# A planner's cost table in a two-layer encoder kernel: GpSimd's rotary steps, the date at which a PSUM bank is free, and the rotation's times

## The chip, the core and the metric

The kernel runs on one core of a Trainium2 chip. The metric is device microseconds of one launch. TensorE (PE in the profile) multiplies into PSUM, which has eight banks of 512 float32 per partition here; VectorE (DVE), ScalarE (ACT) and GpSimd (POOL) do the rest, and SyncE (SP) issues most transfers. Each engine works through its own instructions in the order in which they were written.

## The reference

One sequence of 256 tokens with width 1024 goes through two layers. Each layer is: half a SwiGLU step, a mixer, half a SwiGLU step.

```python
x = x + 0.5 * swiglu(rmsnorm(x, ffn1_norm[i]), gate, up, down)       # D_FF = 2816
h = rmsnorm(x, mix_norm[i])
q_s, k_s, v_s, q_m = split(h @ w_in[i])                              # 12 heads of 64, and 4 memory heads
k_m, v_m = split(rmsnorm(mem, mem_norm[i]) @ w_mem_kv[i])
o_m = memory_attention(headnorm(q_m), headnorm(k_m), v_m)            # 256 memory rows
# layer 0: chunked attention with a learned relative bias; layer 1: differential attention
q, k = headnorm(q_s), headnorm(k_s)
if i == 1:
    q, k = apply_rope(q, cos, sin), apply_rope(k, cos, sin)          # cos, sin from int32 positions
    a = softmax(q0 k0) - lam * softmax(q1 k1)
x = x + concat(o_s, o_m) @ w_out[i]
x = x + 0.5 * swiglu(rmsnorm(x, ffn2_norm[i]), gate, up, down)
```

All of it is float32. Sine and cosine of the positions are wanted in layer 1 only.

## The kernel before

**Products.** A float32 product is made of three passes on rounded operands: high by high, high by low, low by high (L596, L599, L602, helper `dense`; the text calls them dense matmuls). Weights come from DRAM in 1 MB pieces into one of three raw buffers (`raw`, L368). ScalarE casts a piece into its high part (`hi`, L417), VectorE subtracts to get the low part (`lo`, L438), 512 columns at a time, into one of four buffers each. A raw buffer is free for the next load only when VectorE has made the last low part of it.

**Stages.** Layer 0: FFN1, then the key and value products of the memory for both layers (`memory_kv`, operands `memh`, `meml`), then mixer 0 (five projections `proj`, attention, output product), FFN2. Layer 1 the same with mixer 1 and no memory products. After FFN1 of layer 0 the new x goes into transposed form by a way through DRAM (`prep_dram`: `xb` on VectorE, transfer `xd<-xb`, transfer `xr<-xd`, both issued from ScalarE's queue); elsewhere TensorE transposes it (L632).

**Norms.** The inverse root of a norm is a power on GpSimd (L639): `xr` for a block of x rows, `hf` for heads (4 or 8 columns), `of` for outputs, `mr` for memory rows. `xrh` is half of `xr`. The head norm (`head_norm`) is a square on ScalarE (`sq`, L1118), a sum and a scaling on VectorE, the power, and one product on VectorE (`qkn` for q and k, `kmn` for memory keys), which TensorE then transposes. The bias tiles of layer 0 get a memset on GpSimd (L1431) once their load is there.

**The rotary table.** `rope_setup` works out cos and sin of position times frequency. The argument is reduced by 92 small GpSimd steps on 128x64 tiles in `ropew` (L1328 to L1336 in a chain, each needing the one before). Two sines on ScalarE follow (L1367, L1368), then sixteen small products on VectorE (L1377, L1379) into `ropeC` and `ropeS`. An Exp of the lambda sums (`le`, L1407) stands behind the sines, and `nlam` on VectorE behind it. In layer 1, `qk_evac` rotates each block: two GpSimd products (L1471), one VectorE product (L1474), one sum (L1478, tile `m`), transposes.

**What sets the order.** The program is written by a planner that runs at build time. `Flow` keeps a clock `now`, which TensorE's instructions advance, and for ScalarE, VectorE and GpSimd (A, V, G) the time at which each will be free. Stages are generators: each writes an instruction, charges its engine with a duration (`flow.act`, `flow.dve`, `flow.pool`), and yields the time at which the result will be there, 0.14 us (`HOP_E`) behind the charge; it is taken up again when the clock has passed that time. So the charges decide where in each engine's order an instruction is written, and nothing else: on the chip, semaphores see to the real dependencies. `Banks` hands out PSUM banks; a stage that wants one waits until one is free. `g2` and `g4` are pools of SBUF tiles that work alike. A function table is loaded on ScalarE (ACT_TABLE_LOAD) where the function in use changes set; `table_hint` (L1111) does this early for Silu and Exp.

Of the kernel before, what the change touches and what calls it, by code (L numbers as in the profile page):

```python
# [12 lines left out]
F32 = mybir.dt.float32  # L13
# [7 lines left out]
P = 128  # L21
# [29 lines left out]
class Flow:  # L51
# [1 line left out]


    def __init__(self):
        self.now = 0.0
        self.free = {"A": 0.0, "V": 0.0, "G": 0.0}
        self.threads = []
        self.idle = []
# [6 lines left out]
        return self.now + HOP  # L66

    def eng(self, e, dur):
        self.free[e] = max(self.free[e], self.now) + dur
        return self.free[e] + HOP_E  # L70

    def act(self, n, extra=0.0):
# [35 lines left out]

    def _advance(self, limit=None):
        c = [th[0] for th in self.threads + self.idle if not callable(th[0])] + list(self.free.values())  # L110
        c = [t for t in c if t > self.now]
        if limit is not None:
            c.append(limit)
        assert c, "no step left to take"
        self.now = min(c)
# [55 lines left out]
class Banks:  # L171

    def __init__(self, tile):
        self.tile, self.free, self.held = tile, list(range(8)), {}

    @property
    def left(self):
        return len(self.free)  # L180

    def has(self, n=1):
        return lambda: len(self.free) >= n

    def has_pair(self):
        return lambda: any(b + 1 in self.free for b in self.free)

    def _hold(self, view, bs):
        for b in bs:
            self.free.remove(b)  # L190
        self.held[id(view)] = (view, bs)
        return view

    def take(self, shape):
        b = self.free[0]
        n = math.prod(shape[1:])
        view = self.tile[:, b, 0:n]
        if len(shape) == 3:
            view = view.rearrange("p (a c) -> p a c", a=shape[1])
        return self._hold(view, (b,))  # L200

    def take_pair(self):
        age = self.free.index
        b = min((b for b in self.free if b + 1 in self.free), key=lambda b: max(age(b), age(b + 1)))
        return self._hold(self.tile[:, b:b + 2, :], (b, b + 1))

    def give(self, view):
        self.free += self.held.pop(id(view))[1]


@with_exitstack
def kernel(
# [13 lines left out]
    flow = Flow()  # L226
# [8 lines left out]
    pp = ctx.enter_context(tc.tile_pool(name="pp", bufs=1, space=PSUM))  # L235

    dram = ctx.enter_context(tc.tile_pool(name="dram", bufs=4, space=bass.MemoryType.DRAM))
    banks = Banks(pp.tile([P, 8, 512], F32, name="banks"))
    g4 = Slots(flow, gp, "g", 12)
    g2 = Slots(flow, t2, "t", NT2)  # L240
    ctx.enter_context(tc.manual_schedule())
# [487 lines left out]
    def prep_rstd(xt, tb):  # L729
        s = small([P, 1], "sst")  # L730
        nc.vector.tensor_add(s, xt.ss[tb][:, 0:1], xt.ss[tb][:, 1:2])
        flow.dve(1, 0.15)
        yield from rsqrt(xt.r[tb], s, 1, 1.0 / D)
        xt.rt[tb] = flow.now
        nc.gpsimd.tensor_scalar(out=xt.rh[tb], in0=xt.r[tb], scalar1=0.5, scalar2=None, op0=ALU.mult)
        flow.pool(0.25)

    final = []

# [565 lines left out]
    def rope_setup():  # L1305
        n = 64
        pi = const.tile([P, 2], I32, name="pos_i")
        later(pi, positions[0].rearrange("(b p) -> p b", p=P))
        invf = const.tile([P, 32], F32, name="invf")
        later(invf, inv_freq.partition_broadcast(P))  # L1310
        gq = const.tile([P, 2, HD], F32, name="gqk")
        later(gq[:, 0], b_q_norm[0].partition_broadcast(P))
        later(gq[:, 1], b_k_norm[0].partition_broadcast(P))
        yield from loaded()
        yield g2.has()
        w = g2.take([P, 8, n], F32, "ropew")
        ang, hi, lo, acc, a, b, fa, cs = (w[:, i, :] for i in range(8))
        pf = const.tile([P, 2], F32, name="pos_f")
        nc.gpsimd.tensor_copy(pf, pi)
        yield flow.pool(0.25)  # L1320
        for tb in range(2):
            nc.gpsimd.tensor_scalar(out=ang[:, tb * 32:(tb + 1) * 32], in0=invf, scalar1=pf[:, tb:tb + 1],
                                    scalar2=None, op0=ALU.mult)
            yield flow.pool(0.25)
        hr = const.tile([P, n], F32R, name="ropehr")
        nc.scalar.copy(out=hr, in_=ang)
        yield flow.act(n)
        nc.gpsimd.tensor_copy(hi, hr.bitcast(F32))  # L1328
        yield flow.pool(0.25)
        nc.gpsimd.tensor_sub(lo, ang, hi)  # L1330
        yield flow.pool(0.25)

        def frac(dst, src):
            nc.gpsimd.tensor_scalar(out=b, in0=src, scalar1=MAGIC, scalar2=MAGIC, op0=ALU.add, op1=ALU.subtract)  # L1334
            yield flow.pool(0.25)
            nc.gpsimd.tensor_sub(dst, src, b)  # L1336
            yield flow.pool(0.25)

        left = Fraction(TWO_PI_INV_NUM, TWO_PI_INV_DEN)
        first = True  # L1340
        for piece in range(5):
            e2 = 14 + 12 * piece
            cval = Fraction(round(left * (1 << e2)), 1 << e2)
            left -= cval
            for part in (hi, lo):
                nc.gpsimd.tensor_scalar(out=a, in0=part, scalar1=float(cval), scalar2=None, op0=ALU.mult)
                yield flow.pool(0.25)
                nc.gpsimd.tensor_scalar(out=fa, in0=a, scalar1=2.0 ** -12, scalar2=MAGIC, op0=ALU.mult, op1=ALU.add)
                yield flow.pool(0.25)
                nc.gpsimd.tensor_scalar(out=fa, in0=fa, scalar1=MAGIC, scalar2=4096.0, op0=ALU.subtract, op1=ALU.mult)  # L1350
                yield flow.pool(0.25)
                nc.gpsimd.tensor_sub(a, a, fa)
                yield flow.pool(0.25)
                if first:
                    yield from frac(acc, a)
                    first = False
                else:
                    yield from frac(fa, a)
                    nc.gpsimd.tensor_add(acc, acc, fa)
                    yield flow.pool(0.25)  # L1360
                    yield from frac(acc, acc)
        S2PI = 6.283185
        nc.gpsimd.tensor_scalar(out=a, in0=acc, scalar1=0.25, scalar2=None, op0=ALU.add)
        yield flow.pool(0.25)
        yield from frac(a, a)
        sn = fa
        nc.scalar.activation(sn, acc, AF.Sin, scale=S2PI)  # L1367
        nc.scalar.activation(cs, a, AF.Sin, scale=S2PI)  # L1368
        sines.append(flow.act(n, 0.3))
        yield sines[0]  # L1370
        for j, sc in ((0, HD ** -0.5), (1, 1.0)):
            for tb in range(2):
                for hf in range(2):
                    own = slice(hf * 32, hf * 32 + 32)
                    oth = slice(32 - hf * 32, 64 - hf * 32)
                    tt = slice(tb * 32, (tb + 1) * 32)
                    nc.vector.scalar_tensor_tensor(out=ropeC[:, tb, j, own], in0=gq[:, j, own], scalar=sc,  # L1377
                                                   in1=cs[:, tt], op0=ALU.mult, op1=ALU.mult)
                    nc.vector.scalar_tensor_tensor(out=ropeS[:, tb, j, own], in0=gq[:, j, oth],  # L1379
                                                   scalar=-sc if hf == 0 else sc,  # L1380
                                                   in1=sn[:, tt], op0=ALU.mult, op1=ALU.mult)
                    flow.dve(n, 0.06)
                    t = flow.dve(n, 0.06) + 0.3
                    yield lambda: flow.now >= t and flow.free["V"] <= flow.now + SLACK
        g2.give()
# [28 lines left out]
    def mixer(l, xt, gc_next):  # L1414
# [34 lines left out]
        class Heads:  # L1449
            def __init__(self):  # L1450
                self.t = [None, None]
                self.k = None

        def qk_evac(c):
            def run(ps, tb, t):
# [5 lines left out]
                if not typ_a:  # L1461
# [6 lines left out]
                    for hf in range(2):  # L1468
# [4 lines left out]
                            in1=ropeS[:, tb, :, own].unsqueeze(2).broadcast_to([P, 2, 4, 32]), op=ALU.mult)  # L1473
                    nc.vector.tensor_tensor(out=m1v, in0=n4,  # L1474
                                            in1=ropeC[:, tb].unsqueeze(2).broadcast_to([P, 2, 4, HD]), op=ALU.mult)
                    flow.dve(512)
                    yield flow.pool(2.1)
                    nc.vector.tensor_add(m1, m1, m2)  # L1478
                    g2.give(2)
                    nat = m1  # L1480
# [5 lines left out]
                else:  # L1486
# [4 lines left out]
                    for j in range(4):  # L1491
                        t = turn(tp[:, j, :], nat[:, j * P:(j + 1) * P])
# [7 lines left out]
                if tb == 0:  # L1500
                    qk.k = g4.take([P, 2, 2, SEQ], F32R, f"k{c}")
                    qk.f = f = g2.take([P, 2, 2, P], F32, f"qk{c}")
                    if typ_a:
# [13 lines left out]
                else:  # L1517
                    qk.q = g2.take([P, 2, 2, P], F32R, f"q{c}")
                    _, t = yield from split_evac(((a4(qk.k[:, 0, :, ts_]), a4(qk.k[:, 1, :, ts_])), tp[:, 2:4], gk),
                                                 ((a4(qk.q[:, 0]), a4(qk.q[:, 1])), tp[:, 0:2], gq))  # L1520
# [110 lines left out]
        def attn_soft(passes, done, vsrc, vready, grp, tb, bias_t, nk):  # L1631
# [5 lines left out]
            for e in range(2):  # L1637
                s, t = ss[e]
# [26 lines left out]
            yield t  # L1665
            rs = small([P, 4], "rs")
            nc.vector.reciprocal(out=rs, in_=sums)
            flow.dve(4)
            pts = [None, None]
            for e in range(2):  # L1670
                pe = pes[e][0]
# [37 lines left out]
        def attn_diff(passes, done, vsrc, vready, grp, tb, nk):  # L1709
# [22 lines left out]
            yield t  # L1732
            rs = small([P, 4], "rs")
            nc.vector.reciprocal(out=rs, in_=sums)
            flow.dve(4, 0.15)
            cf = small([P, 2], "cf")
            nc.vector.scalar_tensor_tensor(out=cf, in0=sums[:, 0:2], scalar=nlam, in1=rs[:, 2:4],
                                           op0=ALU.mult, op1=ALU.mult)
# [288 lines left out]
```

## Time and profile before

| what | value |
|---|---|
| median of 3 runs | 951.9 us (950.87 to 952.27) |
| the profiled execution | 952.73 us |
| its span | 950.8 us |
| busy: TensorE, VectorE, ScalarE, GpSimd | 939.5, 820.6, 582.2, 110.1 us |
| DMA | 209.27 MB, mean 220 GB/s |
| granted TensorE clock, mean | 0.996 |

The span runs from the first to the last instruction; 1.9 us of the execution lie around it. Times in rows of the timeline count from the span's start. A row of the timeline has the start, the length, engine, line, operation and tiles, and in brackets how long the engine was idle before and what ended that. A dense matmul is shown longer (0.39 us) than the distance to the next one, since they overlap, so what matters on TensorE is the distance from start to start.

### The profile page before, as it was taken

What the parts mean: (1) busy time and instruction counts of PE and PEld (TensorE: products, weight loads), DVE (VectorE), ACT (ScalarE), POOL (GpSimd) and SP (SyncE); (2) the same over time, 40 slices, a digit from 0 to 9 for tenths busy, and PEclk for the clock granted to TensorE, in tenths of its full rate; (3) what the DMA queues carried; (4) which work ended last, traced back from release to release, by engine and by line L of the source; (5) the groups of instructions that cost most, each with busy time, mean ns of one, the idle gap of its engine ahead of it and who ended that gap; (6) DMA issues with size and microseconds to landing.
All of it is one profiled execution on the core that took longest, in us unless ns stands there. A gap on an engine that the chain in (4) does not pass through costs nothing.

```text
span 950.8 us, 13163 instructions
## 1 busy us (share of the span) xinstructions
PE 939.5 (99%) x4445; PEld 771.2 (81%) x4445; DVE 820.6 (86%) x1378; ACT 582.2 (61%) x1087; POOL 110.1 (12%) x170
## 2 busy tenths in 40 slices
PE   9999999989999999999999999999999999999998
PEld 7888888767878888888888888888787788888887
DVE  6988969589998889988888999797989888998896
ACT  6655567367777656557645656564677865655661
POOL 1000048522210000000000000000325100000000
PEclk9999999989999999999999999999999999999999
DMA  9877798389746367796747779775632377589651
GB/s 298 271 251 238 233 341 290 122 280 296 242 152 217 124 220 249 238 319 209 229 132 226 235 227 296 242 243 161 218 120 90 102 242 232 184 273 305 219 185 53
DMA packets 176830, 209.27 MB, mean 220 GB/s; under 512 B 12601, under 2 KB 150650, under 8 KB 176762
## 3 DMA queue, kind: packets, MB, share of 16 engines
q1 hardware_dynamic: 168378, 202.92, 65.5%
q10 hardware_dynamic: 8384, 5.51, 1.8%
q8 instruction: 35, 0.57, 0.3%
q14 instruction: 33, 0.27, 0.1%
HBM read 191.62 MB, written 16.78 MB: 219 GB/s over the span
## 4 chain that ended last, share of the span: by engine, by line
PE 76%; DVE 10%; DMA 5%; POOL 5%; issue 2%; ACT 1%; SPq 1%; ACTq 0%; DVEq 0%
PE banks L596 22%; PE banks L602 22%; PE banks L599 22%; DVE lo L438 4%; PE banks L632 2%; PE banks L619 2%; DMA raw<-in_ffn_w_up_dram 2%; POOL ropew L1334 1%; PE banks L1604 1%; PE banks L625 1%; PE banks L1696 1%; POOL ropew L1336 1%; DMA xr<-xd 1%; ACT hi L417 1%; SPq L368 1%
## 5 line engine op out<-in xcount | busy, mean ns | idle before, releaser
L438 DVE TENSOR_TENSOR lo<-raw,hi 128x512 fp32r<-128x512 f32 (+1 forms) x466 | 388.9, 871 | 44.1 <-ACT hi L417 43.8
L417 ACT CAST hi<-raw 128x512 fp32r<-128x512 f32 (+1 forms) x465 | 333.8, 768 | 148.2 <-PE banks L602 68.2
L596 PE MATMUL banks<-hi,xh 128*128 128x512 f32 x736 | 288.8, 392 | 0.0
L599 PE MATMUL banks<-lo,xh 128*128 128x512 f32 x736 | 288.0, 391 | 0.5 <-DVE lo L1921 0.5
L602 PE MATMUL banks<-hi,xl 128*128 128x512 f32 x736 | 287.3, 390 | 0.0
L599 PEld LDWEIGHTS banks<-lo,xh 128*128 128x128 f32 x736 | 138.4, 188 | 29.1 <-DVE lo L1921 1.0
L596 PEld LDWEIGHTS banks<-hi,xh 128*128 128x128 f32 x736 | 138.3, 188 | 28.6
L602 PEld LDWEIGHTS banks<-hi,xl 128*128 128x128 f32 x736 | 138.3, 188 | 28.5
L596 PE MATMUL banks<-hi,ht 128*128 128x512 f32 x270 | 105.4, 390 | 0.0
L599 PE MATMUL banks<-lo,ht 128*128 128x512 f32 x270 | 105.3, 390 | 0.0
L602 PE MATMUL banks<-hi,ht 128*128 128x512 f32 x270 | 105.2, 390 | 0.0
L417 ACT CAST hi<-wsum 128x1024 fp32r<-128x1024 f32 (+1 forms) x51 | 44.6, 890 | 29.6 <-DVE wsum L430 29.4
L639 POOL TENSOR_TENSOR xr<-v,nhalf 128x1 f32<-128x1 f32 x12 | 8.5, 711 | 454.4 <-DVE v L637 454.3
L596 PEld LDWEIGHTS banks<-hi,ht 128*128 128x128 f32 x270 | 50.7, 188 | 10.5
L602 PEld LDWEIGHTS banks<-hi,ht 128*128 128x128 f32 x270 | 50.7, 188 | 10.4
L599 PEld LDWEIGHTS banks<-lo,ht 128*128 128x128 f32 x270 | 50.7, 188 | 10.4
L805 ACT ACTIVATE sil<-banks,xr 128x256 f32<-128x256 f32 x72 | 33.8, 470 | 35.6 <-PE banks L602 33.4
L438 DVE TENSOR_TENSOR lo<-wsum,hi 128x1024 fp32r<-128x1024 f32 (+1 forms) x51 | 50.7, 1021 | 2.9 <-ACT hi L417 2.4
L838 ACT CAST ht<-hr 128x512 fp32r<-128x512 f32 x34 | 21.0, 616 | 34.0 <-DMA hr<-hd 34.0
L639 POOL TENSOR_TENSOR hf<-v,nhalf 128x8 f32<-128x8 f32 (+1 forms) x20 | 32.0, 1598 | 72.6 <-DVE v L637 72.6
L840 DVE TENSOR_TENSOR ht<-hr,ht 128x512 fp32r<-128x512 f32 x34 | 23.4, 688 | 15.9 <-ACT ht L838 15.9
L430 DVE TENSOR_TENSOR wsum<-raw,wsum 128x512 f32<-128x512 f32 (+1 forms) x36 | 32.4, 919 | 0.3
(223 smaller groups left out, 1263.7 us busy)
## 6 DMA issues: line engine op xcount, KB each, us to landing
raw<-in_ffn_w_down_dram SPq DMA_DIRECT2D x176, 256.0 KB, 4.1
raw<-in_ffn_w_gate_dram SPq DMA_DIRECT2D x81, 512.0 KB, 4.3
raw<-in_ffn_w_up_dram SPq DMA_DIRECT2D x81, 512.0 KB, 5.0
raw<-in_w_in_dram SPq DMA_DIRECT2D x32, 512.0 KB, 4.9
hd<-hb SPq DMA_DIRECT2D x44, 256.0 KB, 5.0
hr<-hd SPq DMA_DIRECT2D x44, 256.0 KB, 4.8
raw<-in_w_out_dram SPq DMA_DIRECT2D x8, 1024.0 KB, 4.8
raw<-in_w_mem_kv_dram SPq DMA_DIRECT2D x4, 1024.0 KB, 5.9
```

Source lines behind the costliest of these rows:

```text
L417: nc.scalar.copy(out=it.part(0, q, w), in_=src())
L430: nc.vector.tensor_sub(it.t[j], x(), y())
L438: nc.vector.tensor_sub(it.part(1, q, w), src(), it.part(0, q, w).bitcast(F32))
L596: nc.tensor.matmul(out=ps, lhsT=xh, rhs=wh, start=start, stop=False)
L599: nc.tensor.matmul(out=ps, lhsT=xh, rhs=wl, start=False, stop=False)
L602: nc.tensor.matmul(out=ps, lhsT=xl, rhs=wh, start=False, stop=stop)
L619: nc.tensor.matmul(out=ps, lhsT=xt.h[tb][:, kk, :], rhs=w, start=start and k == i == 0, stop=False)
L632: nc.tensor.transpose(out=dst, in_=src, identity=ident)
L639: nc.gpsimd.tensor_tensor(out=dst, in0=v[:, :n], in1=nhalf[:, :n], op=ALU.pow)
L805: nc.scalar.activation(sil[:, tb], ps[:, tb, 0:256], AF.Silu, scale=xt.r[tb])
L838: nc.scalar.copy(out=hi, in_=src)
L840: nc.vector.tensor_sub(lo, src, hi.bitcast(F32))
```

## The change

Three groups of edits, all in the planner; every engine gets the same arithmetic as before.

1. In `rope_setup`, and for `xrh`, each small GpSimd step is charged 0.56 us instead of 0.25.
2. `Flow` notes the end of the last charge made (`done`). A bank that is given back is free from that date on, not at once, and `free` lists only banks whose date has passed.
3. The rotation in layer 1 is charged 0.35 us more on VectorE and 2.4 instead of 2.1 on GpSimd; two reciprocals 0.1 and 0.3 more.

```diff
     def eng(self, e, dur):
-        self.free[e] = max(self.free[e], self.now) + dur
+        self.done = self.free[e] = max(self.free[e], self.now) + dur
         return self.free[e] + HOP_E
...
-    def __init__(self, tile):
-        self.tile, self.free, self.held = tile, list(range(8)), {}
+    def __init__(self, flow, tile):
+        self.flow, self.tile, self.held = flow, tile, {}
+        self.given = [(b, 0.0) for b in range(8)]
+
+    @property
+    def free(self):
+        return [b for b, t in self.given if t <= self.flow.now]
...
     def give(self, view):
-        self.free += self.held.pop(id(view))[1]
+        self.given += [(b, self.flow.done) for b in self.held.pop(id(view))[1]]
...
         nc.gpsimd.tensor_copy(pf, pi)
-        yield flow.pool(0.25)
+        yield flow.pool(0.56)
...
-                    flow.dve(512)
-                    yield flow.pool(2.1)
+                    flow.dve(512, 0.35)
+                    yield flow.pool(2.4)
...
-            flow.dve(4)
+            flow.dve(4, 0.1)
...
-            flow.dve(4, 0.15)
+            flow.dve(4, 0.45)
```

The first order changes behind the down products of layer 0's FFN1. Line numbers from the banks on are 4 higher after the change (L1367 is L1371, L417 is L421, L632 is L636). Outside the two mixers and the stretch ahead of mixer 0 the rows are the same.

On ScalarE the two sines stood between memory splits (`memh`) and the switch to Exp, ahead of the first split of the memory weights (`raw_1647`):

```order
L417 CAST hi_0_1719<-raw_1565 128x512 x2
L1212 ACTIVATE memh_1713<-mr,gcol 128x256
L1212 ACTIVATE memh_1714<-mr,gcol 128x256 x2
L1367 ACTIVATE ropew<-ropew 128x64
L1368 ACTIVATE ropew<-ropew 128x64
L1111 ACT_TABLE_LOAD
L1111 ACTIVATE dummy<-dummy 128x1
L1212 ACTIVATE memh_1714<-mr,gcol 128x256
L417 CAST hi_0_1793<-raw_1647 128x512
```

Now they stand in mixer 0, between the squares of the first q and k block's two row halves (`sq`), with a table load ahead of them and another ahead of `le`:

```order
L1122 ACTIVATE sq<-banks,xr 128x512
L421 CAST hi_0_2240<-raw_2131 128x512
L1282 ACTIVATE km_1896<-kr,gcol 128x256
L421 CAST hi_0_2240<-raw_2131 128x512
L1282 ACTIVATE km_1896<-kr,gcol 128x256
L421 CAST hi_0_2240<-raw_2131 128x512 x2
L1371 ACT_TABLE_LOAD
L1371 ACTIVATE ropew<-ropew 128x64
L1372 ACTIVATE ropew<-ropew 128x64
L1122 ACTIVATE sq<-banks,xr 128x512
L1411 ACT_TABLE_LOAD
L1411 ACTIVATE le<-le 128x2
```

So the sines and `le` moved past the memory splits, the transfers of the DRAM way and the casts of nine weight pieces.

On GpSimd all rotary steps stood ahead of the first `xr` of mixer 0, and the head norms of the memory and of q and k behind them without a step between:

```order
L1363 TENSOR_SCALAR ropew<-ropew 128x64
L1334 TENSOR_SCALAR ropew<-ropew 128x64
L1336 TENSOR_TENSOR ropew<-ropew 128x64
L639 TENSOR_TENSOR xr<-v,nhalf 128x1
L735 TENSOR_SCALAR xrh<-xr 128x1
L639 TENSOR_TENSOR xr<-v,nhalf 128x1
L735 TENSOR_SCALAR xrh<-xr 128x1
L1431 MEMSET bias_1939 64x4x64
L639 TENSOR_TENSOR hf<-v,nhalf 128x4
L1431 MEMSET bias_2012 64x4x64
```

Now 34 of the steps stand between them; the last rows of the chain are these:

```order
L643 TENSOR_TENSOR hf<-v,nhalf 128x4
L1340 TENSOR_TENSOR ropew<-ropew 128x64
L1363 TENSOR_TENSOR ropew<-ropew 128x64
L1338 TENSOR_SCALAR ropew<-ropew 128x64
L1340 TENSOR_TENSOR ropew<-ropew 128x64
L1367 TENSOR_SCALAR ropew<-ropew 128x64
L1338 TENSOR_SCALAR ropew<-ropew 128x64
L643 TENSOR_TENSOR hf<-v,nhalf 128x8
L1340 TENSOR_TENSOR ropew<-ropew 128x64
L643 TENSOR_TENSOR hf<-v,nhalf 128x8 x5
```

The sines' argument is complete one step behind the first `hf` of 128x8.

On TensorE, late in mixer 0, the transposes of the softmax (`pe`), three groups of attention products (L1696, with `tr` or `PT`) and the memory scores (L1604) stood in one piece inside the output product:

```order
L632 MATMUL banks<-ident,pe 128x128 x16
L1696 MATMUL banks<-tr,V_2292 64x128 x2
L1696 MATMUL banks<-tr,V_2293 64x128 x2
L1696 MATMUL banks<-tr,V_2292 64x128 x2
L1696 MATMUL banks<-tr,V_2293 64x128 x2
L1696 MATMUL banks<-PT,vm_1943 64x128 x8
L1696 MATMUL banks<-PT,V_2292 64x128 x2
L1696 MATMUL banks<-PT,V_2293 64x128 x2
L1696 MATMUL banks<-PT,V_2292 64x128 x2
L1696 MATMUL banks<-PT,V_2293 64x128 x2
L1604 MATMUL banks<-km_1942,qmT 128x256 x12
L596 MATMUL banks<-hi_0_2708,oT_2923 128x512
```

Now the groups stand apart, with dense matmuls between; two of them:

```order
L636 MATMUL banks<-ident,pe 128x128 x4
L1700 MATMUL banks<-PT,vm_1897 64x128 x8
L600 MATMUL banks<-hi_0_2852,oT_2947 128x512
L603 MATMUL banks<-lo_0_2853,oT_2947 128x512
L606 MATMUL banks<-hi_0_2852,oT_2947 128x512
L600 MATMUL banks<-hi_0_2852,oT_2947 128x512
L603 MATMUL banks<-lo_0_2853,oT_2947 128x512
L606 MATMUL banks<-hi_0_2852,oT_2947 128x512
L636 MATMUL banks<-ident,pe 128x128 x4
L1700 MATMUL banks<-PT,V_2275 64x128 x2
L1700 MATMUL banks<-PT,V_2276 64x128 x2
```

The dense matmuls keep their own order; the groups between them moved by a few dense matmuls.

More of the change, by code (lines that the diff above doesn't have):

```diff
@@ L55, in __init__ @@
     def __init__(self):
-        self.now = 0.0
+        self.now = self.done = 0.0
         self.free = {"A": 0.0, "V": 0.0, "G": 0.0}
@@ L110, in _advance @@
         c = [th[0] for th in self.threads + self.idle if not callable(th[0])] + list(self.free.values())
-        c = [t for t in c if t > self.now]
+        c = [t for t in c + [self.done] if t > self.now]
         if limit is not None:
@@ L182, in has @@
     def has(self, n=1):
-        return lambda: len(self.free) >= n
+        return lambda: self.left >= n
     def has_pair(self):
@@ L188, in _hold @@
     def _hold(self, view, bs):
-        for b in bs:
-            self.free.remove(b)
+        self.given = [g for g in self.given if g[0] not in bs]
         self.held[id(view)] = (view, bs)
@@ L194, in take @@
     def take(self, shape):
-        b = self.free[0]
+        b = (self.free or [g[0] for g in self.given])[0]
         n = math.prod(shape[1:])
@@ L202, in take_pair @@
     def take_pair(self):
-        age = self.free.index
-        b = min((b for b in self.free if b + 1 in self.free), key=lambda b: max(age(b), age(b + 1)))
+        free = self.free if self.has_pair()() else [g[0] for g in self.given]
+        b = min((b for b in free if b + 1 in free), key=lambda b: max(free.index(b), free.index(b + 1)))
         return self._hold(self.tile[:, b:b + 2, :], (b, b + 1))
     def give(self, view):
-        self.free += self.held.pop(id(view))[1]
+        self.given += [(b, self.flow.done) for b in self.held.pop(id(view))[1]]
 @with_exitstack
@@ L237 @@
     dram = ctx.enter_context(tc.tile_pool(name="dram", bufs=4, space=bass.MemoryType.DRAM))
-    banks = Banks(pp.tile([P, 8, 512], F32, name="banks"))
+    banks = Banks(flow, pp.tile([P, 8, 512], F32, name="banks"))
     g4 = Slots(flow, gp, "g", 12)
@@ L735, in prep_rstd @@
         nc.gpsimd.tensor_scalar(out=xt.rh[tb], in0=xt.r[tb], scalar1=0.5, scalar2=None, op0=ALU.mult)
-        flow.pool(0.25)
+        flow.pool(0.56)
     final = []
@@ L1323, in rope_setup @@
                                     scalar2=None, op0=ALU.mult)
-            yield flow.pool(0.25)
+            yield flow.pool(0.56)
         hr = const.tile([P, n], F32R, name="ropehr")
@@ L1328, in rope_setup @@
         nc.gpsimd.tensor_copy(hi, hr.bitcast(F32))
-        yield flow.pool(0.25)
+        yield flow.pool(0.56)
         nc.gpsimd.tensor_sub(lo, ang, hi)
-        yield flow.pool(0.25)
+        yield flow.pool(0.56)
         def frac(dst, src):
             nc.gpsimd.tensor_scalar(out=b, in0=src, scalar1=MAGIC, scalar2=MAGIC, op0=ALU.add, op1=ALU.subtract)
-            yield flow.pool(0.25)
+            yield flow.pool(0.56)
             nc.gpsimd.tensor_sub(dst, src, b)
-            yield flow.pool(0.25)
+            yield flow.pool(0.56)
         left = Fraction(TWO_PI_INV_NUM, TWO_PI_INV_DEN)
@@ L1346, in rope_setup @@
                 nc.gpsimd.tensor_scalar(out=a, in0=part, scalar1=float(cval), scalar2=None, op0=ALU.mult)
-                yield flow.pool(0.25)
+                yield flow.pool(0.56)
                 nc.gpsimd.tensor_scalar(out=fa, in0=a, scalar1=2.0 ** -12, scalar2=MAGIC, op0=ALU.mult, op1=ALU.add)
-                yield flow.pool(0.25)
+                yield flow.pool(0.56)
                 nc.gpsimd.tensor_scalar(out=fa, in0=fa, scalar1=MAGIC, scalar2=4096.0, op0=ALU.subtract, op1=ALU.mult)
-                yield flow.pool(0.25)
+                yield flow.pool(0.56)
                 nc.gpsimd.tensor_sub(a, a, fa)
-                yield flow.pool(0.25)
+                yield flow.pool(0.56)
                 if first:
@@ L1359, in rope_setup @@
                     nc.gpsimd.tensor_add(acc, acc, fa)
-                    yield flow.pool(0.25)
+                    yield flow.pool(0.56)
                     yield from frac(acc, acc)
@@ L1363, in rope_setup @@
         nc.gpsimd.tensor_scalar(out=a, in0=acc, scalar1=0.25, scalar2=None, op0=ALU.add)
-        yield flow.pool(0.25)
+        yield flow.pool(0.56)
         yield from frac(a, a)
```

## The prediction

> **What bounds the kernel now.** The page first: how busy each engine is, and in which slices TensorE is not.
>
> ```profile
> span 950.8 us, 13163 instructions
> PE 939.5 (99%) x4445; PEld 771.2 (81%) x4445; DVE 820.6 (86%) x1378; ACT 582.2 (61%) x1087; POOL 110.1 (12%) x170
> PE   9999999989999999999999999999999999999998
> ```
>
> TensorE works nearly all the time, so the change can only win where TensorE stands still or runs slowly; the one low slice inside the span is around 190 us. The table by stretches opens that place (columns: length, then busy us and instruction count of PE, PEld, DVE, ACT, POOL, then granted clock, DMA share, GB/s).
>
> ```profile
> 160.00:170.00 10.00, 10.00 (x45) 8.26 (x44) 10.00 (x24) 8.16 (x18) 8.68 (x17) 1.00 0.76 268
> 170.00:181.00 11.00, 11.00 (x50) 9.12 (x49) 2.87 (x8) 0.52 (x3) 8.88 (x23) 1.00 0.35 131
> 181.00:188.00 7.00, 6.64 (x30) 5.20 (x29) 5.57 (x16) 5.08 (x10) 0.00 (x0) 1.00 0.00 1
> 188.00:200.00 12.00, 8.42 (x25) 6.03 (x25) 11.06 (x28) 6.59 (x16) 0.83 (x2) 0.72 0.88 292
> 200.00:212.00 12.00, 11.08 (x46) 8.22 (x46) 9.37 (x21) 6.96 (x15) 3.60 (x6) 1.00 0.79 242
> 212.00:240.00 28.00, 27.37 (x125) 22.24 (x124) 26.33 (x56) 20.81 (x42) 7.82 (x6) 1.00 0.93 301
> ```
>
> Read down the columns. From 170 to 181 VectorE and ScalarE almost stop while GpSimd alone works; from 181 to 188 the DMA engines carry nothing; from 188 to 200 TensorE loses matmuls and its granted clock falls to 0.72. The waits of ScalarE and VectorE between 160 and 200 say what the first stop was.
>
> ```profile
> ACT ropew L1367 <- POOL ropew L1336: 10.1, 1, 10.1
> DVE ropeC L1377 <- ACT ropew L1368: 8.1, 1, 8.1
> ```
>
> ScalarE reached the sine of the rotary table (L1367) 10.1 us before GpSimd had finished its argument, and everything behind it in ScalarE's order waited: the casts L417 that split the next weights. VectorE sat behind the sines at L1377. Raw buffers came free late, so no load was issued, and TensorE paid last:
>
> ```profile
> 188.79 0.40 PE L602 MATMUL banks<-hi,meml 128*128 128x512 f32 x1
> 191.99 0.79 PE L596 MATMUL banks<-hi,memh 128*128 128x512 f32 x1 [2.81 <-ACT hi L417]
> 193.56 0.79 PE L599 MATMUL banks<-lo,memh 128*128 128x512 f32 x1 [0.77 <-DVE lo L438]
> 194.15 0.63 PE L602 MATMUL banks<-hi,meml 128*128 128x512 f32 x1
> 194.57 0.63 PE L596 MATMUL banks<-hi,memh 128*128 128x512 f32 x1
> ```
>
> After 2.81 us without work the matmuls start 0.42 us apart (194.15 to 194.57), where 45 in 10 us (row 160:170) means 0.22.
>
> **The change, part by part.**
>
> *Rotary steps at 0.56 us instead of 0.25.* The pace GpSimd really had, first and last step before the sines:
>
> ```profile
> 128.91 0.52 POOL L1328 COPY ropew<-ropehr 128x64 f32<-128x64 f32 x1 [14.24 <-ACT ropehr L1326]
> 180.36 0.32 POOL L1336 TENSOR_TENSOR ropew<-ropew 128x64 f32<-128x64 f32 x1
> ```
>
> From the first's start to the last's end are 92 steps (and two short powers for the memory rows) in 51.8 us, 0.56 each. The planner took 0.25 plus its hop of 0.14 per step and so put the sines too early. With 0.56 plus the hop it puts them far later: in the new order they stand behind the first 128x8 `hf` of the first q/k block, in mixer 0, and not before its memory products. No arithmetic is added or removed on GpSimd.
>
> What the stall costs: at the rate of 160 to 181 ((45 + 50) / 21 = 4.52 matmuls a us) the 31 us from 181 to 212 would hold 140; they held 30 + 25 + 46 = 101. 39 missing matmuls are 8.7 us, half-clock time included. I take all of it: **-8.7**. The lower bound is the part before 200 alone: 19 us would hold 86, they held 55, 6.8 us.
>
> Where do the sines block now? In the new order GpSimd has 34 rotary steps left from the mixer's first `xr`, spread between two `xr`, three bias memsets and five `hf` (four of 128x4).
>
> ```profile
> 191.09 0.57 POOL L639 TENSOR_TENSOR xr<-v,nhalf 128x1 f32<-128x1 f32 x1 [10.40 <-DVE v L637]
> 226.97 2.05 POOL L639 TENSOR_TENSOR hf<-v,nhalf 128x8 f32<-128x8 f32 x1 [3.94 <-DVE v L637]
> L639 POOL TENSOR_TENSOR hf<-v,nhalf 128x4 f32<-128x4 f32 x8 | 9.5, 1186 | 28.5 <-DVE v L637 28.5
> 216.56 0.31 POOL L1431 MEMSET bias<- 64x256 f32 x1 [3.63 <-PE banks L602]
> ```
>
> From the start of that `xr` to the end of that `hf` there are 37.9 us. The steps beside a busy VectorE (row 160:170: 17 in 10 us) take 0.59 each, so 34 are 20 us; two `xr` some 1.2, four `hf` 4.8, the long one 2.1, memsets 0.9: 29 us of 37.9. The tightest part is the last: the third memset at 216.56 waits for TensorE, and from there to 226.97, 10.4 us, stand 11 steps (6.5) and two short `hf` (2.4). So the argument is ready about when `hf` is, plus one last step, and ScalarE reaches the sines after four casts and two `km` activations. ScalarE's wait there: 0 to 0.5 us.
>
> New work on ScalarE: in the old order the sines stood before the switch to Exp, now they stand after it, and the new order has two table loads more (before the sine, before `le`).
>
> ```profile
> 181.00 1.28 ACT L1111 ACT_TABLE_LOAD   x1
> 182.29 0.20 ACT L1111 ACTIVATE dummy<-dummy 128x1 f32<-128x1 f32 x1
> 211.90 0.62 ACT L417 CAST hi<-raw 128x512 fp32r<-128x512 f32 x1 [2.34 <-DMA raw<-in_w_in_dram]
> 229.85 0.66 PE L632 MATMUL banks<-ident,qkn 128*128 128x128 f32 x4 [0.63 <-DVE qkn L1127]
> ```
>
> Two loads are 2.6 us, which the planner does not reckon. Their cover is the lead of the splits: at 211.90 a cast came 2.34 us late in this mixer, and TensorE's only wait from 212 to 240 is the 0.63 before L632, which is no wait for a split. If that cover is gone, they cost up to 2.6. `le` now also holds `nlam` on VectorE, with five splits and the second `qkn` queued behind it; that block's transposes keep their place among the dense matmuls. I put **+0.8** for ScalarE's and VectorE's new lateness, between 0 and 2.6, nearer to 0 because the late cast cost nothing. The Trainium skill, "ScalarE: Activation LUTs", section "What ACT_TABLE_LOAD costs", adds about 1.38 us of drain to each load; here the next instruction starts 1.29 after the load's start, so the row decides. By that page the two loads would be about 5.3 us (an estimate), and the sum up to 2.7 us worse.
>
> The 0.63 itself should go: the first `qkn` transposes now stand seven dense matmuls (1.5 us) later. **-0.6**, at worst 0.
>
> *Rotation in layer 1 (512 with 0.35 more on VectorE, 2.4 for the GpSimd pair), reciprocals (+0.1, +0.3).*
>
> ```profile
> PE banks L632 <- DVE m L1478: 0.7, 2, 0.4
> PE banks L632 <- DVE oT L1569: 0.2, 1, 0.2
> L1474 DVE TENSOR_TENSOR m<-qkn,ropeC x6: 685/774/1232, 682.0 to 728.7; 128x512 f32<-128x512 f32 x6
> L1471 POOL TENSOR_TENSOR m<-qkn,ropeS x12: 738/1059/1454, 681.7 to 729.2; 128x256 f32<-128x256 f32 x12
> ```
>
> All waits of TensorE between 660 and 800 are 0.9 us. Two `ropeS` products at 1.06 are 2.1 us and can reach 2.4; the first two rotation transposes move two and one dense matmuls back. That covers the 0.4 and part of the rest: **-0.5**, from 0 to -0.9.
>
> *A bank free when its reader is done.* The only bank wait that could be meant is the 0.2 at L1569. In `finish` and `prep_half` the bank is given back before the reader is charged, so there the date noted is an older instruction's; it does nothing there. What the new dates do is move small groups of products: with fewer banks at once, groups that ran in one piece are run apart. In the new order the dense stream is broken by scores or AV products 12 times instead of 9 in mixer 0, and 15 instead of 12 in mixer 1. One break's price, an AV group (16 by the profile's count) alone and the same inside a run:
>
> ```profile
> 294.53 1.04 PE L1696 MATMUL banks<-PT,vm 128*64 128x128 f32 x16
> 295.41 1.04 PE L1696 MATMUL banks<-PT,V 128*64 128x128 f32 x16
> ...
> 304.96 0.40 PE L602 MATMUL banks<-hi,oT 128*128 128x512 f32 x1
> 305.28 1.09 PE L1696 MATMUL banks<-PT,vm 128*64 128x128 f32 x16
> 306.31 0.50 PE L596 MATMUL banks<-hi,oT 128*128 128x512 f32 x1
> ```
>
> Alone it takes 1.35 from the last dense start to the next, less one dense pitch of 0.22: 1.13, and the dense matmul behind it is 0.1 longer; in the run 0.88. So about 0.3 a break, six of them **+1.8** (0 if the groups' inner waits are the same, 2.1 at 0.35 each).
>
> Sum: -8.7 - 0.6 - 0.5 + 0.8 + 1.8 = **-7.2**. The profiled execution took 952.7 (span 950.8 and 1.9 around it); that gives 945.5. It lies 0.8 above the median of the runs shown, 951.9, so I forecast **944.7** for the median.
>
> **The rivals.**
>
> *The wait only moves.* ScalarE waits for GpSimd again, now in mixer 0. From the sums above it begins where 11 steps fill 10.4 - 2.4 = 8 us, 0.73 a step, and over the whole way at 28.9 / 34 = 0.85, against 0.59 measured beside the busiest VectorE. At 1.0 a step the sines are 5 us late; taking off the 2.3 us of lead seen, TensorE idles about 2.8, the gap after which the clock fell above, and loses another 2 or more there: 4 to 5 us back, **949**.
>
> *The round trip through DRAM is the real limit.* ScalarE's order also holds the issue of `xr<-xd`, which waits until `xd<-xb` has landed.
>
> ```profile
> 190.40 6.12 DMA xd<-xb
> 196.54 7.37 DMA xr<-xd
> ACT hi L417 <- DMA xd<-xb: 2.8, 1, 2.8
> ```
>
> From the chain: 6.1 out and 7.4 back, under the rush of loads after 188. If the four trips hold ScalarE 2.8 each in 176 to 196, some 3 us of the 8.7 stay: **947.7**. Against it: without the stop, the trips start about 10 us earlier and the loads come spread out.
>
> *Slower.* GpSimd's steps delay the `hf` queued behind them. In-order as it is, each `hf` of the memory keys and of q/k stands behind two to six rotary steps. To eat 7.2 us, they would have to run some 7 + 2.3 us late: 38 us for 34 steps, 1.1 us each. The Trainium skill, "GPSIMD Engine Reference", section "Key points", has GpSimd share its SBUF interfaces with VectorE and names VectorE instructions with two SBUF inputs, which the splits L438 are. The trace agrees in kind: 23 operations in 8.88 us busy beside an idle VectorE (row 170:181), 17 in 8.68 beside a full one, 0.39 against 0.51 each; 1.1 lies far above both. Time: **954**.
>
> *It changes nothing.* The planner moves the sines but something else late at 188 holds TensorE, as above: 951.5.
>
> **How the numbers follow.** The forecast has 0.70 (own range 942 to 947.3), the wait that moves 0.09, the round trip 0.11, no change 0.05, slower 0.05. The range holds the forecast, the round trip and most of the moved wait: 941.7 to 949. About 0.2% (1.9 us) is what a measurement here can tell from no change; 0.90 of the cases lie below that, 0.05 within, 0.05 above.
>
> **What would show it.** In the new profile ScalarE's wait at the sine (L1371 there) is under 1 us, DMA has no empty stretch between 170 and 190, and the memory products run from 186 to 208 at 4.5 a us with the clock at 1.00: that is the -8.7. Two more ACT_TABLE_LOAD, 7 in all. More than 1 us of TensorE waits on `qkn`, L421 or L442 between 200 and 235 would spoil the +0.8; as many matmuls a us as before in the rest of both mixers would say that the breaks cost nothing. A wait of ScalarE on GpSimd or on `xd` above 3 us, or a clock below 1.00 after 200, would make the forecast wrong.

## The result, and the profile after

The changed kernel takes 944.43 us (median of 6 runs, 942.75 to 945.40); the kernel before, on the same chip, 952.19 (6 runs, 950.87 to 954.47). The ratio is 0.9912, 95% interval 0.9897 to 0.9927. A second comparison, beside three experiments below, gave 943.11 and 0.9898 (0.9885 to 0.9912). The profiled execution took 944.51 us.

The page first, with the same lines as before:

```profile
span 942.6 us, 13176 instructions
PE 936.2 (99%) x4445; PEld 768.8 (82%) x4445; DVE 821.4 (87%) x1378; ACT 583.5 (62%) x1089; POOL 112.9 (12%) x170
PE   9999999999999999999999999999999999999998
```

The low slice around 190 is gone. The same stretches as in the prediction (length, busy us and count of PE, PEld, DVE, ACT, POOL, granted clock, DMA share, GB/s):

```profile
170.00:181.00 11.00, 11.00 (x50) 9.13 (x49) 9.66 (x21) 4.45 (x11) 5.50 (x14) 1.00 0.59 187
181.00:188.00 7.00, 7.00 (x32) 5.79 (x32) 3.42 (x5) 2.22 (x6) 3.08 (x9) 1.00 0.70 246
188.00:200.00 12.00, 12.00 (x54) 9.94 (x54) 10.10 (x19) 9.15 (x19) 5.93 (x12) 1.00 0.88 284
200.00:212.00 12.00, 11.50 (x50) 8.89 (x49) 11.93 (x25) 7.72 (x16) 7.31 (x12) 1.00 0.77 258
212.00:240.00 28.00, 27.91 (x140) 22.50 (x139) 27.17 (x81) 24.67 (x57) 9.08 (x12) 1.00 0.79 255
```

VectorE works on from 170 to 181, the DMA engines carry 246 GB/s from 181 to 188 where they carried 1, and the clock from 188 to 200 is 1.00 where it was 0.72. Of the waits that the prediction asked about, these are left (total, times, longest):

```profile
ACT ropew L1372 <- POOL ropew L1340: 0.9, 1, 0.9
PE banks L603 <- DVE lo L442: 0.5, 2, 0.3
PE banks L636 <- DVE m L1482: 0.2, 1, 0.2
```

ScalarE waits 0.9 us between the two sines instead of 10.1 ahead of them; TensorE waits on no `qkn`, and 0.2 us on the rotation where its waits between 660 and 800 were 0.9 in all. The profile has seven table loads, as the prediction said.

**Where the time went.** The dense matmuls stand in the same order in all fourteen profiles of this study (thirteen kernels, the changed one twice), so each stage can be timed from the start of its first dense matmul to the start of the next stage's first. The memory products are dense matmuls 780 to 875 (counted from 0), mixer 0 is 876 to 1211, mixer 1 is 2658 to 2993. Every stage outside these took the same in every kernel: 179.4 to 180.2 us ahead (from the first dense matmul), 342.0 between the mixers, 161.6 behind (to the start of the last dense matmul). So the whole study is in this table (us, one profiled execution each).

| kernel | pace | banks | rotation | memory products | mixer 0 | mixer 1 | span |
|---|---|---|---|---|---|---|---|
| before | | | | 30.7 | 111.0 | 114.5 | 950.8 |
| after; again | x | x | x | 22.8; 21.8 | 111.5; 111.2 | 113.7; 113.7 | 942.6; 941.2 |
| p1_pace | x | | | 21.8 | 112.7 | 114.6 | 943.4 |
| p2_banks | | x | | 31.6 | 112.3 | 116.2 | 954.7 |
| p3_rotation | | | x | 27.5 | 111.7 | 116.5 | 950.1 |
| p13_pace_rotation | x | | x | 22.0 | 112.5 | 116.5 | 945.5 |
| late_sines | | | | 22.9 | 110.6 | 114.6 | 942.4 |
| pace40 | 0.40 | x | x | 24.3 | 110.8 | 113.8 | 944.6 |
| four_loads | x | x | x | 25.1 | 116.0 | 113.7 | 949.1 |
| slow_steps | x | x | x | 23.3 | 117.0 | 113.8 | 948.6 |
| sines_ffn2 | x | x | x | 21.8 | 112.2 | 113.8 | 942.1 |
| sines_ffn2_quarter | 0.25 | x | x | 23.6 | 112.0 | 113.8 | 944.1 |
| sines_ffn2_nobanks | x | | x | 23.6 | 112.1 | 116.5 | 946.7 |

The change is -7.9 in the memory products, +0.5 in mixer 0, -0.8 in mixer 1: -8.2 of span (in its second profile -8.9, +0.2 and -0.8). The eleven profiles without the stall spread from 21.8 to 25.1 in the memory products, and the two of one kernel lie 1.0 apart, so a difference of that size in this column says nothing.

### The profile page after: what moved, and what is told of

It is laid out like the page before. It is cut to its first block, busy times and chain, and to the rows that moved or that the text cites. A ratio compares the mean times of both kernels' runs of the same rounds, so it can differ in the third digit from the quotient of the medians.

```text
span 942.6 us, 13176 instructions
## 1 busy us (share of the span) xinstructions
PE 936.2 (99%) x4445; PEld 768.8 (82%) x4445; DVE 821.4 (87%) x1378; ACT 583.5 (62%) x1089; POOL 112.9 (12%) x170
## 4 chain that ended last, share of the span: by engine, by line
PE 92%; DVE 5%; DMA 1%; ACT 1%; issue 1%; POOL 0%; ACTq 0%
PE banks L606 28%; PE banks L600 28%; PE banks L603 28%; PE banks L636 2%; PE banks L623 2%; DVE lo L442 2%; PE banks L1608 1%; PE banks L629 1%; PE banks L1700 1%; DMA xr<-xd 1%; ACT hi L421 0%; POOL hf L643 0%; PE banks L1757 0%; DVE m L1478 0%; DVE hss L1125 0%
## 5 line engine op out<-in xcount | busy, mean ns | idle before, releaser
L442 DVE TENSOR_TENSOR lo<-raw,hi 128x512 fp32r<-128x512 f32 (+1 forms) x466 | 390.6, 873 | 48.9 <-ACT hi L421 48.5
L421 ACT CAST hi<-raw 128x512 fp32r<-128x512 f32 (+1 forms) x465 | 333.8, 768 | 145.5 <-PE banks L606 74.7
L421 ACT CAST hi<-wsum 128x1024 fp32r<-128x1024 f32 (+1 forms) x51 | 44.6, 890 | 28.7 <-DVE wsum L434 28.5
L442 DVE TENSOR_TENSOR lo<-wsum,hi 128x1024 fp32r<-128x1024 f32 (+1 forms) x51 | 50.4, 1020 | 3.1 <-ACT hi L421 2.8
```

The source lines that it names most:

```text
L421: nc.scalar.copy(out=it.part(0, q, w), in_=src())
L442: nc.vector.tensor_sub(it.part(1, q, w), src(), it.part(0, q, w).bitcast(F32))
```

## The experiments

**The parts of the change, one at a time.** Each kernel is the one before with some of the three groups of edits, as in the diff above: the pace alone, the bank dates alone, the rotation and reciprocals alone, and pace with rotation.

> Of the change only the rotary steps at 0.56 us; banks and rotation times as before. Theory (the sines no longer stop ScalarE, and that is the whole gain): 8 us below the kernel before, 944 to 945, sines' wait on ScalarE under 1.5 us, no DMA gap at 181. Rival (the dates of the banks or the rotation's times carry a part): only 5 to 6 us below, 946 to 947. In its order mixer 0 has 12 breaks of the dense stream like the changed kernel, mixer 1 has 12 like the kernel before: if a break costs 0.3 us, this one gains up to 0.9 on the changed kernel in mixer 1.

> Of the change only the dates of the banks; rotary steps at 0.25 and rotation as before. The order has as many breaks as before (9 and 12), so the breaks do not come from the banks, against what the prediction said. Theory: within 1 us of the kernel before, 951 to 953, with the 10 us wait at the sines still there. Rival (bank dates spare TensorE waits of their own): 1 to 2 us faster.

> Of the change only the rotation and reciprocal times. Theory: the waits at the rotation's transposes shrink by 0.5 us, 3 more breaks in mixer 1 and 2 in mixer 0 cost up to 1.5: 951.5 to 953.5. Rival (the breaks cost nothing, the waits go): 0.5 to 1 us faster, 951 to 951.5.

> The change without the dates of the banks. Theory: like the changed kernel within 0.5 us, 944 to 945. Rival (bank dates matter beside the other two): 946 or more.

Measured against the kernel before on the same chip (median 951.79):

| kernel | median | ratio (95%) |
|---|---|---|
| p1_pace | 945.34 | 0.9938 (0.9924 to 0.9952) |
| p2_banks | 955.66 | 1.0045 (1.0028 to 1.0062) |
| p3_rotation | 954.51 | 1.0032 (1.0021 to 1.0043) |
| p13_pace_rotation | 947.66 | 0.9964 (0.9952 to 0.9975) |

The profiled execution of p3_rotation, 951.85 us, is the fastest of its ten, so its row in the table shows its good end. The pace alone is most of the gain; its time lies between what its theory and its rival had. The other two parts, each alone, make the kernel slower, by more than theory or rival had for either. Without the dates the rival came true: they matter beside the other two. The profiles of the pace alone, the banks alone and the rotation alone, in this order, say first that only the pace takes the stall away (where ScalarE still waits 8.3 to 11.2 us at the sine, the memory products take 27.5 to 31.6 us):

```profile
ACT ropew L1368 <- POOL ropew L1336: 0.3, 1, 0.3
```

```profile
ACT ropew L1371 <- POOL ropew L1340: 11.2, 1, 11.2
188.00:200.00 12.00, 7.94 (x24) 5.72 (x25) 11.65 (x28) 5.87 (x14) 0.83 (x2) 0.72 0.82 267
746.65 0.41 PE L636 MATMUL banks<-ident,o 128*128 128x128 f32 x2 [1.59 <-ACT pe L1663]
```

```profile
ACT ropew L1367 <- POOL ropew L1336: 8.3, 1, 8.3
PE banks L632 <- ACT pe L1659: 1.5, 1, 1.5
PE banks L632 <- ACT PT L1618: 0.5, 1, 0.5
```

Their last lines are the second finding. Mixer 1 takes 114.5 or 114.6 in all kernels with neither banks nor rotation, 116.5 in all with the rotation and no dates, 116.2 with the banks alone, and 113.7 or 113.8 in all seven profiles with both: +2.0, +1.7, and together -0.8. The timeline of pace with rotation shows what the rotation brings. First TensorE, then ScalarE:

```profile
733.85 0.40 PE L602 MATMUL banks<-hi,oT 128*128 128x512 f32 x1
735.78 0.44 PE L632 MATMUL banks<-ident,o 128*128 128x128 f32 x2 [1.53 <-ACT pe L1659]
735.97 0.48 PE L596 MATMUL banks<-hi,oT 128*128 128x512 f32 x1
736.28 0.40 PE L599 MATMUL banks<-lo,oT 128*128 128x512 f32 x1
736.52 0.39 PE L602 MATMUL banks<-hi,oT 128*128 128x512 f32 x1
...
741.71 0.66 PE L632 MATMUL banks<-ident,pe 128*128 128x128 f32 x4 [0.50 <-ACT PT L1618]
```

```profile
734.71 0.47 ACT L1659 ACTIVATE pe<-banks,nm 128x256 f32<-128x256 f32 x1
...
735.16 0.47 ACT L1659 ACTIVATE pe<-banks,nm 128x256 f32<-128x256 f32 x1
```

The transposes of `o` do not read `pe`. They write into a bank that the code gives back as soon as the Exp (L1659) is written down (`banks.give(src)` right behind it), and on the chip the Exp runs until 735.6. With the dates on top, the two waits are gone: between 660 and 800 only the 0.2 us of the row above is left. That the dates hand another bank to these transposes is inferred from that. The banks alone still have a wait of 1.59 of the same kind; that a date is only as good as the planned end of the reader would explain it, but no run tests that. In mixer 0, too, the pace alone has a wait of TensorE on an Exp, here at the scores (0.5 with the rotation added); neither profile of the changed kernel has any wait of TensorE there:

```profile
PE banks L1604 <- ACT pe L1659: 0.7, 1, 0.7
```

**The sines late, and nothing else.** The kernel before with one line in `rope_setup`, ahead of the sines; all rotary steps keep 0.25 and their order. The planner writes some later instructions of the other engines in another order too.

```diff
+        yield flow.now + 13.0
         nc.scalar.activation(sn, acc, AF.Sin, scale=S2PI)
```

> The kernel before, with all charges as before, but rope_setup lets 13 us of the planner's clock go by before it writes the two sines, so they stand behind the place where ScalarE waited 10.1 us. Two more table loads, like the changed kernel. Theory (only the sines' place matters, not the pace of the steps or the order of GpSimd): ScalarE's wait at the sine under 2 us, memory products from 185 to about 208, 944 to 946.5. Rival (the stall hangs on GpSimd's steps standing in one block, or on the table load and the way through DRAM): 948 or more.

Measured: 944.73 us, ratio 0.9934 (0.9911 to 0.9958), beside a kernel before of 951.67. The sine in its timeline:

```profile
L1368 ACT ACTIVATE ropew<-ropew x1: 257/257/257, 181.1 to 181.1; 128x64 f32<-128x64 f32 x1
188.00:200.00 12.00, 12.00 (x55) 9.93 (x54) 11.04 (x23) 10.63 (x22) 3.14 (x5) 1.00 0.84 266
```

The first sine starts at 181.1, no earlier than before (179.3, as soon as its argument was there); only, the work that had waited behind it now stands ahead of it, and ScalarE does not wait for GpSimd there. The memory products take 22.9. So the cause of the stall is shown: the sines' place in ScalarE's order, and not the pace as such.

**A smaller pace.** The changed kernel with 0.40 for 0.56 at every step:

```diff
-        yield flow.pool(0.56)
+        yield flow.pool(0.40)
```

> The changed kernel with rotary steps charged 0.40 instead of 0.56. The sines then stand some 20 rows of ScalarE earlier, still behind the memory weights' first casts. Theory (any place later than the argument's real end will do): wait at the sine under 2 us, 944 to 946. Rival (0.56 is needed, the chain is still late): ScalarE waits 3 us or more, 948 or more.

Measured: 943.77 us, ratio 0.9928 (0.9908 to 0.9948). The sines stand at 199.7, without a wait. So 0.56 is not needed: 0.40, too, puts the sines behind their argument.

**Two more table loads.** The changed kernel with two dummy activations behind `le`, which the planner does not reckon:

```diff
         nc.scalar.activation(e, e, AF.Exp)
+        nc.scalar.activation(dummy, dummy, AF.Silu)
+        nc.scalar.activation(dummy, dummy, AF.Exp)
```

> The changed kernel with two more table loads behind le (a Silu and an Exp of one element, not charged to the planner, so that the order of everything else stays). Theory (the splits' lead covers 2.6 us of ScalarE in mixer 0): within 0.7 us of the changed kernel, 944 to 945.2. Rival (no cover left): 2.6 us or more on top, 947 and above, with TensorE waits for L421 or L442 between 215 and 235.

Measured: 947.42 us (10 runs, 945.70 to 951.23), ratio 0.9963 (0.9945 to 0.998). Its profiled execution is the slowest of the ten; 2.1 of its loss lie between 187.9 and 192.7, ahead of the edit, in waits for splits of the memory weights. The other 4.5 us, in mixer 0, are these (ScalarE, VectorE, TensorE):

```profile
226.58 1.28 ACT L1412 ACT_TABLE_LOAD   x1
...
228.10 1.28 ACT L1413 ACT_TABLE_LOAD   x1
...
229.50 2.16 ACT L421 CAST hi<-raw 128x512 fp32r<-128x512 f32 x4
...
230.14 2.50 DVE L442 TENSOR_TENSOR lo<-raw,hi 128x512 fp32r<-128x512 f32 x4 [2.78 <-ACT hi L421]
232.55 0.74 DVE L1131 SCALAR_TENSOR_TENSOR qkn<-banks,xr,hf 128x512 f32<-128x512 f32 x1
...
230.01 0.39 PE L600 MATMUL banks<-hi,xh 128*128 128x512 f32 x1
233.35 1.11 PE L636 MATMUL banks<-ident,qkn 128*128 128x128 f32 x4 [2.96 <-DVE qkn L1131]
...
235.12 0.63 PE L600 MATMUL banks<-hi,xh 128*128 128x512 f32 x1
235.54 0.63 PE L603 MATMUL banks<-lo,xh 128*128 128x512 f32 x1
```

The loads hold four casts, the casts hold four of the five low parts that stand ahead of the second `qkn` on VectorE, and `qkn` holds TensorE for 2.96 us; then the matmuls come 0.42 us apart instead of 0.23. In the changed kernel the same transposes have just no wait:

```profile
227.73 0.74 DVE L1131 SCALAR_TENSOR_TENSOR qkn<-banks,xr,hf 128x512 f32<-128x512 f32 x1
...
228.04 0.39 PE L600 MATMUL banks<-hi,xh 128*128 128x512 f32 x1
228.52 0.66 PE L636 MATMUL banks<-ident,qkn 128*128 128x128 f32 x4
```

`qkn` ends at 228.47 and the transposes start at 228.52, 0.05 later; in four_loads they start 0.06 after the end of theirs (233.29). So nothing was left of the cover here: the two loads of the change fit, and in this execution the next two cost their full length and the clock on top. The rival's time came true, but not its wait: it looked for one of TensorE on a split (L421 or L442), and TensorE waited for `qkn`. Between the medians the price is 3.0 us (947.42 against 944.43), and the fastest of the ten runs is only 1.3 above the changed kernel's median, so 4.5 is not paid every time.

**Every GpSimd step twice.** The changed kernel with a second small step behind nearly every rotary step, without a charge:

```diff
+        nc.gpsimd.tensor_scalar(out=spare, in0=invf, scalar1=0.5, scalar2=None, op0=ALU.mult)
         yield flow.pool(0.56)
```

> The changed kernel with a second small GpSimd product (128x32, into a spare tile, not charged) ahead of each step of the rotary chain's main part, which makes a step 0.95 to 1.1 us instead of 0.56; the order of everything else stays. By the prediction's reckoning the sines are then 5 to 8 us late in mixer 0: ScalarE waits 4 to 8 us there, and the time goes to 948 to 953. Rival (hf and the sines have more room than reckoned): under 946.5.

Measured: 951.44 us, ratio 1.0005 (0.9993 to 1.0017). Its waits from 200 to 240, and TensorE's timeline:

```profile
ACT vm L1258 <- DVE kmn L1131: 10.2, 4, 3.5
DVE kmn L1131 <- POOL hf L643: 6.2, 4, 2.6
PE banks L636 <- DVE qkn L1131: 4.0, 1, 4.0
ACT ropew L1381 <- POOL ropew L1342: 1.2, 1, 1.2
```

```profile
227.31 0.66 PE L636 MATMUL banks<-ident,qkn 128*128 128x128 f32 x4 [4.00 <-DVE qkn L1131]
...
228.50 0.61 PE L600 MATMUL banks<-hi,xh 128*128 128x512 f32 x1
228.90 0.63 PE L603 MATMUL banks<-lo,xh 128*128 128x512 f32 x1
...
231.88 0.41 PE L606 MATMUL banks<-hi,xl 128*128 128x512 f32 x1
```

The expected range of times holds, but not its reason: the sines wait 1.2 us, not 4 to 8, and do no harm. The head norms' powers `hf`, in GpSimd's order behind the steps, come late instead, and `kmn`, `vm`, `qkn` and TensorE with them. That is the mechanism of the rival "slower". Between 213.58 and 218.53 five steps with their doubles took 4.95 us, 0.99 a pair, and at about that pace the gain is eaten up.

**The sines out of mixer 0.** The changed kernel with the sines held back until the switch to Silu behind mixer 0, and `le` no longer tied to them, so that no table load is added; then the same with a pace of 0.25, and the same without the bank dates. The changed kernel ran again beside them.

```diff
         sn = fa
+        yield lambda: len(silu) > 0
...
         table_hint(AF.Silu)
+        silu.append(True)
         g4.give(4)
...
-        yield lambda: len(sines) > 0
+        yield lambda: len(lam_e) > 0
         e = lam_e[0]
-        yield sines[0]
```

> The changed kernel, with the two sines held back until the switch to Silu at the end of mixer 0, and the Exp of the lambda sums no longer tied to them: five table loads instead of seven, no sine and no rotary product of VectorE in the first half of mixer 0. Theory A (ScalarE's extra work in mixer 0 is on the path from the head norm to the transposes, which two further loads made 4.5 us longer in one profile): mixer 0 loses 0.5 to 1.5 us against the changed kernel, median ratio to before 0.990 to 0.9915. Theory B (two loads are still covered, the third and fourth are not): mixer 0 stays at 104 to 105 us, ratio 0.9915 to 0.993, the same as the changed kernel within what can be measured. TensorE's wait on the first qkn below 0.7 us in both.

> As sines_ffn2, but with the GpSimd steps reckoned at 0.25 us again. If it was only the place of the sines that the new pace set right, the time is that of sines_ffn2 within 2 us (ratio 0.990 to 0.993), and the memory products take 22 to 23 us although the planner has the pace wrong by half. If the pace matters by itself, for the order of the head norms behind the steps, it is 2 us or more slower, with a wait on qkn or kmn.

> As sines_ffn2, but with a bank free as soon as it is given back, as before the change. If the dates of the banks are worth what the two earlier kernels with and without them gave (3.2 us between the medians, by two waits of 1.5 and 0.5 us in mixer 1), it is 2 to 3.5 us slower than sines_ffn2, with the waits of the transposes pe and PT on ScalarE back at 735 to 742 us and mixer 1 at 110 to 111 us instead of 108. If that difference was chance, mixer 1 takes 108 to 109 us and the times agree within 1 us.

> The changed kernel beside the other three on the same chip, as their yardstick: ratio 0.990 to 0.993, memory products 22 to 23.5 us, mixer 0 104 to 105.5, mixer 1 107.5 to 108.5.

Measured beside a kernel before of 952.75:

| kernel | median | ratio (95%) |
|---|---|---|
| sines_ffn2 | 944.29 | 0.9917 (0.9902 to 0.9932) |
| sines_ffn2_quarter | 944.41 | 0.9914 (0.9899 to 0.9929) |
| sines_ffn2_nobanks | 947.60 | 0.9938 (0.9921 to 0.9954) |
| after_again | 943.11 | 0.9898 (0.9885 to 0.9912) |

The stage times for the mixers in these recorded texts are 5 to 7 us shorter than those of the table above, so they go by other marks; their differences can still be compared. Theory A falls: without the two loads and the sines, mixer 0 takes 112.2 us, not less than the 111.2 and 111.5 with them. The planner wrote another order there, and the first `qkn` is late again, as before the change; without this wait it would be about 111.5, still no gain:

```profile
PE banks L636 <- DVE qkn L1131: 0.7, 1, 0.7
```

The wrong pace costs nothing that the runs can tell (944.41 against 944.29) once the sines stand elsewhere. The text recorded for sines_ffn2 puts the two further loads on a path from the head norm; the timeline above shows that they go through the casts. And without the dates mixer 1 takes 116.5 again, with the same two waits of 1.5 and 0.5 us:

```profile
PE banks L632 <- ACT pe L1659: 1.5, 1, 1.5
PE banks L632 <- ACT PT L1618: 0.5, 1, 0.5
```

No kernel of this study beats the changed one beyond the uncertainty.

## Why the prediction was right, and where it was not

The forecast for the median was 944.7; 944.43 was measured, and 943.11 in the second comparison. What carries it, the stall and its cause, is right; the nearness of the number is in part luck, as the sum by stages below shows. Step by step:

- **-8.7, the stall:** the memory products lost 7.9 us in the first profile and 8.9 in the second, late_sines (only the sines moved) 7.8. The step and its cause are right. The prediction's own count gives less. It added up rows, and an instruction that crosses an edge stands in both: the rows from 181 to 212 add to 101 before and 136 after, 35 more where the prediction had 39 (as one window 99 and 133). The same work timed from end to end is the cleaner sum.
- **-0.6, the first `qkn`:** the wait is gone in both profiles of the changed kernel. In sines_ffn2 it is back at 0.7.
- **+0.8, new lateness of ScalarE and VectorE:** near 0. TensorE has no wait at all in mixer 0 in either profile of the changed kernel, and sines_ffn2, which takes both loads away, gains nothing. The reason given (a late cast of 2.34 us cost nothing) was a weak one: the path that decides is the one named beside it, five splits ahead of the second `qkn`, and it had nothing to spare.
- **-0.5, the rotation:** TensorE's waits between 660 and 800 fell from 0.9 to 0.2, so -0.7 in the changed kernel. But the edit alone makes mixer 1 2.0 us longer.
- **+1.8, six more breaks of the dense stream:** this step failed in its cause, and in mixer 1 in its size. The breaks do not come from the bank dates: in the order of p2_banks there are 9 and 12, as before; the pace alone brings 12 in mixer 0 (the rotation alone 11), the rotation the 15 of mixer 1. In mixer 1, -0.8 measured and -0.7 of it from waits leaves about -0.1 for three breaks, not +0.9. Mixer 0 is 0.2 to 0.5 longer although its wait of 0.6 is gone; the 0.8 to 1.1 us left over come without any wait of TensorE and are about what the prediction had for three breaks there. That the breaks are what costs them is not shown: p2_banks, with 9, is some 0.7 longer beyond its waits as well.
- **The bank dates,** of which the prediction said that they spare at most the 0.2 at L1569 and otherwise break the stream: wrong. (That they do nothing in `finish` and `prep_half` is untested.) Alone they cost 3.9 us of the median; on top of pace and rotation they are worth 3.3 (944.29 against 947.60), 2.7 of it in mixer 1. The waits that they remove in mixer 1 are not in the profile of before; they come with the rotation edit. Costing each part by the profile of before could not find this.

By stages, the prediction had -8.7 in the memory products, +1.1 in mixer 0 (-0.6, +0.8 and three breaks) and +0.4 in mixer 1 (-0.5 and three breaks); measured were -7.9, +0.5 and -0.8. The sum, -7.2 against -8.2, is as near as it is because the misses have both signs, and that is luck.

The rivals: that the wait moves into mixer 0 did not happen (0.9 us, no TensorE wait behind it). The round trip through DRAM is no limit: in the second profile of the changed kernel ScalarE waits longer on it than before, and the memory products take 21.8 us without any wait of TensorE.

```profile
ACT hi L421 <- DMA xd<-xb: 6.2, 2, 5.7
```

The price of the rival "slower" was a good one: it needed 1.1 us a step to eat up the gain, and slow_steps did it at about 0.99. The rival of the moved wait was wrong to look at the sines: at that pace they hold nothing up, and the head norms do.

What stays open: why the bank dates alone make mixer 0 1.3 us longer, of which one wait that the kernel before does not have is 0.6, and why the runs of four_loads spread over 5.5 us.

```profile
PE banks L636 <- DVE pe L1677: 0.6, 1, 0.6
```

## What to carry to other kernels

In a schedule written out ahead of time, look for the instruction that an in-order engine reaches long before its operand is ready, and price it by what stands behind it: here a 0.26 us sine cost 8 us, and each of the four later places tried, from 181.1 to 310.5 us, gave them back. Corrections of a planner's tables do not add up: two that each cost time alone (3.9 and 2.7 us) gained 0.9 to 2.2 together on top of the third (945.34 against 944.43 and 943.11), so each needs to be tried with the others in place, on stages timed from the same work to the same work. Where a new cost seems covered, follow the queue of every engine behind it to the first wait, and compare ends with starts: here two table loads left TensorE without a wait, and the next two cost 3.0 us of the median, 4.5 in the execution profiled.

## What the runs showed of the hardware

The price of a pause of TensorE jumps with its length. After 2.81 us (before), 2.96 (four_loads) and 4.00 us (slow_steps) without work the matmuls come 0.40 to 0.43 us apart, and the granted clock is 0.50: from 191.14 to 197.97 (6.83 us), from 233.30 to 236.71 and from 228.50 to 231.91 (3.41 us each). So the slow stretch lasted once or twice 3.41 us. Its start is not tied to the pause: in the kernel before the clock fell 2.35 us after the last matmul's start, with the pause still on; in slow_steps it fell only at the fourth dense matmul behind the pause. After the 1.53 us of p13_pace_rotation the next starts are 0.31 us apart (735.97 to 736.28) and then 0.23 to 0.24. The Trainium skill, "TensorE: Matmul & The Clock Gate", section "Why this matters for your kernels", asks for no idle gaps above about 3 us, and its section "What's actually happening" has a free-running activity window of about 3.4 us. The 3.41 us agree with such a window; the gap that sufficed was a little shorter here, 2.81 us. So the 2.96 us cost 4.5, and the 1.53 us little more than themselves.
